# Low parts of the down-projection weights: from a VectorE subtraction to a ScalarE negation and an adding DMA

## The chip, the core and the metric

The kernel runs on one core of one Trainium2 chip. The metric is the device time of one execution in microseconds (us). Engines are named as in the profile: PE (TensorE, matrix products), DVE (VectorE), ACT (ScalarE), POOL (GpSimd) and SP (SyncE, which here issues the DMAs). PEld is PE's load of a stationary operand.

## What is computed

The reference is a trunk of two layers over 512 latent tokens and 256 context tokens with 1024 features, in float32. Each layer has three sub-layers: a SwiGLU feed-forward, a mixer (attention in layer 0, gated linear attention in layer 1) and a second SwiGLU. Cut to what matters here:

```
h = rms_norm(x, norm_g[i]) * (1 + scale) + shift
z = h @ w_gu                      # 1024 -> 2 * 2816
hid = silu(z_gate) * z_up         # 2816 hidden features
x = x + 0.5 * gate * (hid @ w_down)   # 2816 -> 1024
```

There are four such feed-forwards: ffn1 and ffn2 of layer 0, ffn1 of layer 1 (all three over 768 tokens), and ffn2 of layer 1 (over the 512 latent tokens only, the last stage of the kernel). The change concerns `w_down` alone.

## The kernel before, in words

**Numbers.** PE multiplies in a format (float32r) that keeps fewer bits than float32. Every operand is therefore split exactly into a high part `hi` (the value rounded to float32r) and a low part `lo = value - hi`, and each product is made of three: hi by hi, hi by lo, lo by hi (`pair`, L360, records them at L368). In the trace the weights are `whi` and `wlo`, the hidden operand is `dh` and `dl`, and the PSUM regions are `r`, `a` or `b`.

**Loading a weight unit.** `load_split` (L103) loads a unit in two halves. For each half, `raw` (L119) takes one of three buffers of the tag `raw` and issues the load from DRAM on SP's queue (L122). `split` (L125) then makes `whi` with a copy on ACT (L127) and `wlo` with a subtraction on DVE (L128). `whi` and `wlo` have three buffers each. These three rings of three buffers (`raw`, `whi`, `wlo`) are shared by all weights that pass through the feed-forward: a half can be loaded only when the `raw` buffer of three halves earlier has been read for the last time, and it can be converted only when PE has finished with the `whi` and `wlo` of three halves earlier.

**A feed-forward.** The 22 hidden tiles of 128 features are worked in four parts of 6, 6, 5 and 5 tiles (`PARTS`). In each part the gate and up products of its hidden tiles come first. From a hidden tile on that depends on the stage, they are made in seven products of halves (Strassen's form; `unit`, L612, matrix products at L596), whose weights go through the same rings in four pairs of buffers per tile. Then the part's down projection adds to the residual: four units of two halves (`load` at L531, used at L539), where a half holds 128 output features by 5 or 6 hidden tiles, that is 640 or 768 columns. In the first three parts each half is multiplied with all tokens at once. The fourth part is made by `close_out` (L396) in two passes over the tokens, so that the next norm can begin early: the first pass takes 256 tokens, with four units in order; the second pass takes the rest (512 tokens, in the last feed-forward 256), with the units in reverse order, of which the first is still there. So a close loads seven units, 14 halves. With three parts of eight halves before it, a feed-forward loads 38 halves, and the four feed-forwards load 152.

A half of the first pass of a close is only 15 products of 256 columns; a half of a main part is 36 products over 768 tokens (30 where the part has five tiles).

**Beside it.** DVE also adds the gated result to the residual (L392), forms the combinations of the seven products (L618, L633, L642, L652), and makes products for the modulation vectors of later sub-layers in the background (L291, with their own DMAs `wm<-w_mod`). ACT does the copies, Silu and the squares of the norm. POOL works in the two mixers only; it issues no DMA anywhere.

**The order of the work.** The program is written with a tile framework that places the waits. The order of instructions on each engine is not the order of the source: a planner simulates the time line with its own costs and takes what is ready, so a change of one operation's cost or engine can reorder others. Each engine and each DMA queue then works in its fixed order.

Of the kernel before, what the change touches and what calls it, by code (L numbers as in the profile page):

```python
# [14 lines left out]
ALU = mybir.AluOpType  # L15
# [12 lines left out]
ALL_SEGS = [(0, 256), (256, 512), (512, T)]  # context tokens, latent tokens  # L28
# [3 lines left out]
class Stage:  # L32
    """A sub-layer: loads its first weights, one unit after the other, then waits for its operand."""
# [14 lines left out]
class Net:  # L48
# [28 lines left out]
    # ---- the residual: four slots that hold other things inside a mixer, while it waits in DRAM --  # L77
# [25 lines left out]
    def load_split(self, src, n, pool=None, keep=4, slots=(None, None)):  # L103
        """n columns in two halves, each as (hi, lo)"""
# [13 lines left out]

    def raw(self, src):  # L119
        n = src.shape[-1]  # L120
        raw = self.stage.tile([128, 1024], F32, tag="raw", name="raw", bufs=3)[:, :n]
        self.nc.sync.dma_start(out=raw, in_=src)  # L122
        return raw

    def split(self, src, hi, lo, e=None):  # L125
        """src (float32, SBUF) -> hi + lo, both float32r"""
        self.nc.scalar.activation(out=hi, in_=src, func=AF.Copy)  # L127
        (e or self.nc.vector).tensor_tensor(out=lo, in0=src, in1=hi.bitcast(F32), op=ALU.subtract)  # L128

# [1 line left out]
    def rsqrt(self, out, v, shape):  # L131
        """out = 1/sqrt(v) for a small positive float32 tile"""
# [33 lines left out]
    def mod_finish(self, l, p):  # L166
        """bias; the scale piece becomes norm_g * (1 + scale), the FFN gates carry the 1/2"""
# [11 lines left out]
    def first_open(self, pool):  # L179
        """silu(c), silu(c_ctx) and zeros; the sum of four groups of 32 rows"""  # L180
# [14 lines left out]
    def first_product(self, pool, raw):  # L195
        """256 features of the vectors on the tensor engine, four products of 32 columns side by side"""
# [13 lines left out]
    def first_norm(self, pool, m, raw):  # L210
        """shift and scale of the first sub-layer, 128 features"""
# [7 lines left out]
    def first_gate(self, pool, i, raw):  # L219
        """half of the gate of the first sub-layer, 256 features"""  # L220
# [5 lines left out]
    def first_stats(self, pool):  # L226
        """1/rms of all tokens, on every partition"""
# [27 lines left out]
    def mod_queue(self, *pieces):  # L255
        """the products of the pieces (layer, number), in the two halves of the sums"""
# [6 lines left out]
    def mod_half(self, i):  # L263
        """a half of silu(c) and of silu(c_ctx) on every partition, for the background products"""
# [35 lines left out]
    def norm_squares(self, pool, seg, order=range(KT)):  # L300
        """sum over the features of a partition of the squares"""
# [13 lines left out]
    def norm_stats(self, seg, acc):  # L315
        """1/rms of each token of the segment, on every partition (PSUM)"""
# [36 lines left out]
    def mm3(self, out, w, x, first, last):  # L353
        """out += w^T x, w = (hi, lo) stationary, x = (hi, lo) moving"""
# [5 lines left out]
    def pair(self, w, nk, xk, segs, outs, cols=(0, 1)):  # L360
        """two column tiles of a weight unit, w[j] = (hi, lo) of [128, nk * 128], against the
        feature-major operand xk[k] = (hi, lo); outs[seg][j] are PSUM regions"""
# [9 lines left out]
    def regions(self, segs):  # L372
        """PSUM for two column tiles of each segment"""
# [22 lines left out]
    def close_out(self, load, nk, xk, segs, gate, nxt, off=0):  # L396
        """The last products of a sub-layer, in two passes over the weights: the norm of the first tokens runs
        under the products of the others, theirs under the first products of the next sub-layer, whose first
        weights come ahead of all that."""
# [46 lines left out]
    def ffn(self, l, sub, idx, segs, nxt, bg=(0, 0), first=4, start=False):  # L446
# [3 lines left out]
        # the first tiles: without the last segment, under the norm of it  # L450
# [9 lines left out]
        with st:  # L460
# [7 lines left out]
            def up(f, ss, regs=None):  # L468
                """the hidden tile f for the segments ss"""
# [13 lines left out]
            if start:  # L483
                # as the features come
# [28 lines left out]
            for pi, (f0, nf) in enumerate(PARTS):  # L513
# [17 lines left out]
                load = lambda u: self.load_split(dn[u], 2 * nf * 128)  # L531
# [14 lines left out]
    def seven_open(self, st, h, n0):  # L546
        """Gate and up columns (rows 1, 2) of a hidden tile against halves of the features and of the tokens,
        in seven products of halves in place of eight (Winograd's form of Strassen's)."""
# [50 lines left out]
        def start():  # L599
            """the place of the fourth block is free now"""  # L600
# [57 lines left out]
    def bcast(self, ap, n):  # L658
        """[128, a, b] -> [128, a, b, n] with a stride of zero"""
        return ap.unsqueeze(len(ap.shape)).to_broadcast(list(ap.shape) + [n])  # L660

    def rms_scale(self, pool, groups, shape, pool_squares=False):
        """1/rms of each group: groups = list of (ap [128, t, g, d], slice of the stats tile)"""
# [21 lines left out]
    def rope(self, pool, out, x, tab, nh, half):  # L685
        """x, out [128, nh, 2 * half] of one token tile; tab = (cos * gain, sin * gain) [128, 2 * half]"""
# [12 lines left out]
    def rot_tables(self, pool, nm, cos, sin, gain, d):  # L699
        """cos * gain and sin * gain, [128, 4, d]"""  # L700
# [14 lines left out]
    def pair_mixer(self, nxt, l=0):  # L715
        """Window attention of the first key/value head runs between the rest of the input projections,
# [1102 lines left out]
```

## Time and profile before

| | us |
|---|---|
| time, median of 3 runs | 2731.77 (2730.58 to 2735.99) |
| span of the profiled execution | 2731.1 |
| PE busy | 2639.5 (97%) |
| DVE busy | 2171.2 (80%) |
| ACT busy | 1197.9 (44%) |
| POOL busy | 170.3 (6%) |

The profiled execution's span, from its first to its last instruction, is 0.7 us below the median of the runs; its own device time is not listed apart. The busy share of PE counts modelled ends of pipelined matmuls, so the waits and the spacing of instructions say more than the share. The stages by time, in us from the span's start: start and ffn1 of layer 0 to about 572, attention mixer to about 1000, ffn2 of layer 0 and ffn1 of layer 1 to about 2066, gated linear attention and its projections to about 2412, ffn2 of layer 1 to the end. In each line of the trace, L12 is line 12 of the kernel; `out<-in` are the program's names.

### The profile page before, as it was taken

How to read it: one execution, taken by the hardware profiler on the slowest of the kernel's cores; microseconds unless marked ns; L12 is line 12 of the kernel's file. 1: busy time of each engine (PE TensorE's matmuls, PEld its weight loads, DVE VectorE, ACT ScalarE, POOL GpSimd, SP SyncE). 2: the span in 40 equal slices, each digit the busy share in tenths (PEclk: the TensorE clock that was granted, in tenths of full speed). 3: DMA queues.
4: the chain of work that ended last, by engine and by line, in shares of the span. 5: the costliest groups of instructions: out<-in, count | busy, mean ns of one | idle time of the engine just before them, and what ended most of it. 6: DMA issues, size and time to landing. Idle time of an engine off the chain costs nothing. (4 is left out here: it accounts for less than half of the span.)

```text
span 2731.1 us, 44146 instructions
## 1 busy us (share of the span) xinstructions
PE 2639.5 (97%) x16848; PEld 2450.8 (90%) x16848; DVE 2171.2 (80%) x4540; ACT 1197.9 (44%) x2254; POOL 170.3 (6%) x206
## 2 busy tenths in 40 slices
PE   7999999999978899999999999999999999899999
PEld 5899999989867789999999899999998999899899
DVE  5689798977788877797989877978777677778677
ACT  4324242445656753333324542424244555534444
POOL 0000000013344300000000000000000121000000
PEclk9999999999989999999999999999999999999999
DMA  8143444431000050433433314343233112422234
GB/s 311 41 144 119 137 132 143 132 126 31 24 24 1 1 170 24 126 120 122 130 124 110 126 47 144 100 149 105 91 105 102 55 63 70 147 64 97 96 108 130
DMA packets 103461, 279.30 MB, mean 102 GB/s; under 512 B 12146, under 2 KB 15090, under 8 KB 101714
## 3 DMA queue, kind: packets, MB, share of 16 engines
q1 hardware_dynamic: 103250, 276.49, 31.3%
q8 instruction: 132, 2.16, 0.3%
q14 instruction: 79, 0.65, 0.1%
HBM read 269.11 MB, written 7.34 MB: 101 GB/s over the span
## 5 line engine op out<-in xcount | busy, mean ns | idle before, releaser
L127 ACT ACTIVATE whi<-raw 128x512 fp32r<-128x512 f32 (+3 forms) x466 | 356.0, 767 | 730.7 <-PE r L368 324.2
L128 DVE TENSOR_TENSOR wlo<-raw,whi 128x512 fp32r<-128x512 f32 (+3 forms) x466 | 400.1, 861 | 72.3 <-ACT whi L127 69.7
L596 PE MATMUL r<-t,whi 128*128 128x384 f32 (+1 forms) x1704 | 401.2, 323 | 2.8 <-DVE u L633 2.0
L596 PE MATMUL r<-hh,wlo 128*128 128x384 f32 (+1 forms) x1136 | 366.3, 323 | 0.2
L596 PE MATMUL r<-hh,whi 128*128 128x384 f32 (+1 forms) x1136 | 365.8, 322 | 0.0
L596 PE MATMUL r<-hl,whi 128*128 128x384 f32 (+1 forms) x1136 | 365.8, 322 | 0.0
L291 DVE SCALAR_TENSOR_TENSOR junk<-wm,cb 128x512 bf16<-128x512 f32 x480 | 328.8, 685 | 13.1 <-ACT cb L270 8.0
L596 PEld LDWEIGHTS r<-t,whi 128*128 128x128 f32 x1704 | 295.6, 188 | 4.5 <-DVE u L633 2.8
L596 PE MATMUL r<-t,wlo 128*128 128x384 f32 (+1 forms) x852 | 273.3, 323 | 0.2 <-DVE wlo L128 0.2
L368 PE MATMUL r<-dh,whi 128*128 128x512 f32 (+1 forms) x952 | 267.3, 345 | 0.8 <-ACT whi L127 0.8
L368 PE MATMUL r<-dh,wlo 128*128 128x512 f32 (+1 forms) x952 | 266.8, 346 | 0.3 <-DVE wlo L128 0.3
L368 PE MATMUL r<-dl,whi 128*128 128x512 f32 (+1 forms) x952 | 266.8, 344 | 0.0
L127 ACT ACTIVATE whi<-s 128x512 fp32r<-128x512 f32 x284 | 174.9, 625 | 187.5 <-DVE s L618 75.2
L596 PEld LDWEIGHTS r<-hh,wlo 128*128 128x128 f32 x1136 | 213.4, 188 | 1.3 <-DVE wlo L128 1.3
L596 PEld LDWEIGHTS r<-hl,whi 128*128 128x128 f32 x1136 | 213.4, 188 | 0.8
L596 PEld LDWEIGHTS r<-hh,whi 128*128 128x128 f32 x1136 | 213.4, 188 | 0.3
L368 PEld LDWEIGHTS r<-dh,wlo 128*128 128x128 f32 x952 | 178.6, 188 | 24.3 <-DVE wlo L128 1.1
L368 PEld LDWEIGHTS r<-dh,whi 128*128 128x128 f32 x952 | 178.0, 188 | 24.5 <-ACT whi L127 2.7
L368 PEld LDWEIGHTS r<-dl,whi 128*128 128x128 f32 x952 | 178.1, 188 | 23.5
L128 DVE TENSOR_TENSOR wlo<-s,whi 128x512 fp32r<-128x512 f32 x284 | 190.6, 683 | 2.8 <-ACT whi L127 2.1
L392 DVE SCALAR_TENSOR_TENSOR x<-r,mod,x 128x512 f32<-128x512 f32 (+1 forms) x168 | 100.0, 631 | 87.3 <-PE r L368 86.9
L596 PEld LDWEIGHTS r<-t,wlo 128*128 128x128 f32 x852 | 159.9, 188 | 0.5 <-DVE wlo L128 0.5
(403 smaller groups left out, 5880.4 us busy)
## 6 DMA issues: line engine op xcount, KB each, us to landing
raw<-gu SPq DMA_DIRECT2D x176, 512.0 KB, 4.0
wm<-w_mod SPq DMA_DIRECT2D x240, 256.0 KB, 2.9
raw<-dn SPq DMA_DIRECT2D x88, 320.0 KB, 2.9
raw<-dn SPq DMA_DIRECT2D x64, 384.0 KB, 3.1
raw<-w_out SPq DMA_DIRECT2D x28, 512.0 KB, 3.7
m<-w_mod0a SPq DMA_DIRECT2D x12, 1024.0 KB, 10.2
raw<-w_in SPq DMA_DIRECT2D x8, 512.0 KB, 4.5
raw<-w_kq SPq DMA_DIRECT2D x8, 512.0 KB, 3.6
```

What stands on the lines that cost most here:

```text
L127: self.nc.scalar.activation(out=hi, in_=src, func=AF.Copy)
L128: (e or self.nc.vector).tensor_tensor(out=lo, in0=src, in1=hi.bitcast(F32), op=ALU.subtract)
L291: nc.vector.scalar_tensor_tensor(out=junk, in0=w, scalar=1.0, in1=self.cb[:, v, :], op0=ALU.mult, op1=ALU.mult, accum_out=self.acc[:, m, v ...
L368: nc.tensor.matmul(out=outs[s][j], lhsT=w[j][wi][:, k * 128:(k + 1) * 128], rhs=xk[k][xi][:, s0:s1], start=(k == 0 and i == 0), stop=(k == ...
L392: self.nc.vector.scalar_tensor_tensor(out=self.xs[m][:, s0:s1], in0=regs[s][j], scalar=gate[:, m, v:v + 1], in1=self.xs[m][:, s0:s1], op0= ...
L596: nc.tensor.matmul(out=o, lhsT=y[wi], rhs=x[k][xi], start=first and k == 0 and i == 0, stop=last and k == H - 1 and i == 2, skip_group_che ...
```

## The change

The down-projection weights are loaded by a new function, `load_parts`. It takes the same buffers, with the same three of each. The low part is now made by two steps: ACT writes `-hi` (a copy with scale -1.0) into the `wlo` buffer, and a DMA issued by POOL adds the raw weights to it in place, with both its source and its destination in SBUF. ACT then writes `hi` as before. The subtraction on DVE is gone for these halves; all other weights keep `load_split`. The remainder of the diff removes comments and docstrings.

```diff
+    def load_parts(self, src, n):
+        res = []
+        for j in range(2):
+            raw = self.raw(src[:, j * (n // 2):(j + 1) * (n // 2)])
+            hi = self.stage.tile([128, 1024], F32R, tag="whi", name="whi", bufs=3)[:, :n // 2]
+            lo = self.stage.tile([128, 1024], F32R, tag="wlo", name="wlo", bufs=3)[:, :n // 2]
+            self.split_by_dma(raw, hi, lo)
+            res.append((hi, lo))
+        return res
+
+    def split_by_dma(self, src, hi, lo):
+        nc = self.nc
+        nc.scalar.activation(out=lo, in_=src, func=AF.Copy, scale=-1.0)
+        nc.gpsimd.dma_start(out=lo, in_=src, accum_op=ALU.add)
+        nc.scalar.activation(out=hi, in_=src, func=AF.Copy)
...
-                load = lambda u: self.load_split(dn[u], 2 * nf * 128)
+                load = lambda u: self.load_parts(dn[u], 2 * nf * 128)
```

## Rows read from the trace of the kernel before

**Rows 1.** Page, part 1: busy us, share of the span, instructions.

```profile
span 2731.1 us, 44146 instructions
PE 2639.5 (97%) x16848; PEld 2450.8 (90%) x16848; DVE 2171.2 (80%) x4540; ACT 1197.9 (44%) x2254; POOL 170.3 (6%) x206
```

**Rows 2.** Stretches: busy us of PE, PEld, DVE, ACT, POOL; PE clock, DMA share, GB/s.

```profile
515.00:540.00 25.00, 23.25 (x148) 22.23 (x147) 22.22 (x52) 11.73 (x20) 0.00 (x0) 0.93 0.49 149
800.00:830.00 30.00, 20.00 (x95) 16.10 (x94) 29.73 (x82) 13.17 (x34) 15.93 (x16) 0.66 0.12 36
1120.00:1180.00 60.00, 60.00 (x346) 53.77 (x345) 47.16 (x105) 12.08 (x18) 0.00 (x0) 1.00 0.43 137
2704.00:2714.00 10.00, 10.00 (x87) 10.00 (x86) 7.05 (x13) 3.31 (x5) 0.00 (x0) 1.00 0.81 248
```

**Rows 3.** PE's waits for VectorE, whole span: us in total, times, longest.

```profile
PE b L368 <- DVE dl L128: 2.4, 4, 1.2
...
PE r L596 <- DVE u L633: 2.0, 3, 1.1
...
PE b L368 <- DVE hl L344: 1.6, 2, 0.8
```

**Rows 4.** Instruction groups by form: busy us, mean ns of one, idle before, releasers.

```profile
L128 DVE TENSOR_TENSOR wlo<-raw,whi 128x640 fp32r<-128x640 f32 x88 | 71.7, 820 | 19.7 <-ACT whi L127 18.9
...
L128 DVE TENSOR_TENSOR wlo<-raw,whi 128x768 fp32r<-128x768 f32 x68 | 65.1, 960 | 11.5 <-ACT whi L127 10.5
...
L127 ACT ACTIVATE whi<-raw 128x640 fp32r<-128x640 f32 x88 | 64.3, 738 | 144.5 <-PE r L368 61.9 <-PE r L596 32.6 <-PE b L368 20.1
...
L127 ACT ACTIVATE whi<-raw 128x768 fp32r<-128x768 f32 x68 | 57.2, 846 | 208.8 <-PE r L368 170.6 <-PE r L596 27.5 <-issue 7.3
```

**Rows 5.** ScalarE in order of time, second part of ffn2, layer 0: main halves.

```profile
1282.07 0.85 ACT L127 ACTIVATE whi<-raw 128x768 fp32r<-128x768 f32 x1 [5.43 <-PE r L368]
1288.35 0.85 ACT L127 ACTIVATE whi<-raw 128x768 fp32r<-128x768 f32 x1 [5.43 <-PE r L368]
```

**Rows 6.** ScalarE in order of time: second pass of the first close, then the last close.

```profile
554.09 0.74 ACT L127 ACTIVATE whi<-raw 128x640 fp32r<-128x640 f32 x1 [1.44 <-PE a L368]
...
557.57 0.74 ACT L127 ACTIVATE whi<-raw 128x640 fp32r<-128x640 f32 x1 [2.74 <-PE a L368]
...
2706.63 0.74 ACT L127 ACTIVATE whi<-raw 128x640 fp32r<-128x640 f32 x1 [1.53 <-DMA raw<-dn]
2708.80 0.74 ACT L127 ACTIVATE whi<-raw 128x640 fp32r<-128x640 f32 x1 [1.43 <-DMA raw<-dn]
2710.35 0.74 ACT L127 ACTIVATE whi<-raw 128x640 fp32r<-128x640 f32 x1 [0.81 <-DMA raw<-dn]
2714.56 0.74 ACT L127 ACTIVATE whi<-raw 128x640 fp32r<-128x640 f32 x1 [3.47 <-PE b L368]
2716.32 0.74 ACT L127 ACTIVATE whi<-raw 128x640 fp32r<-128x640 f32 x1 [1.03 <-PE b L368]
2718.09 0.74 ACT L127 ACTIVATE whi<-raw 128x640 fp32r<-128x640 f32 x1 [1.03 <-PE b L368]
```

**Rows 7.** DMA issues, KB each, us to landing, and the queue's share of 16 engines.

```profile
q1 hardware_dynamic: 103250, 276.49, 31.3%
...
raw<-dn SPq DMA_DIRECT2D x88, 320.0 KB, 2.9
...
x<-x_t SPq DMA_DIRECT2D x4, 768.0 KB, 7.5
...
ident<-ident SPq DMA_DIRECT2D x1, 64.0 KB, 2.3
```

**Rows 8.** The weight loads' issues on SP: duration ns min/median/max.

```profile
L122 SPq DMA_DIRECT2D raw<-dn x152: 327/328/383, 127.8 to 2718.1; - x152
```

**Rows 9.** VectorE and PE in order of time: main part's first half; two closes' second.

```profile
1258.47 0.95 DVE L128 TENSOR_TENSOR wlo<-raw,whi 128x768 fp32r<-128x768 f32 x1
...
1264.08 0.51 PE L368 MATMUL r<-dh,wlo 128*128 128x256 f32 x2
...
524.35 0.81 DVE L128 TENSOR_TENSOR wlo<-raw,whi 128x640 fp32r<-128x640 f32 x1
...
527.62 0.28 PE L368 MATMUL b<-dh,wlo 128*128 128x256 f32 x1
...
2696.96 0.82 DVE L128 TENSOR_TENSOR wlo<-raw,whi 128x640 fp32r<-128x640 f32 x1 [1.51 <-ACT whi L127]
...
2699.46 0.28 PE L368 MATMUL b<-dh,wlo 128*128 128x256 f32 x1
```

**Rows 10.** VectorE and PE in order of time: first half, part two, last feed-forward.

```profile
2531.18 0.96 DVE L128 TENSOR_TENSOR wlo<-raw,whi 128x768 fp32r<-128x768 f32 x1 [0.69 <-ACT whi L127]
...
2532.19 0.50 PE L368 MATMUL r<-dh,wlo 128*128 128x512 f32 x1 [0.26 <-DVE wlo L128]
```

## The prediction, made before the kernel was run

> **What bounds the kernel now.** I read the page first [rows 1]: PE 97% busy, DVE 80%, ACT 44%. That invites the thought that DVE is the next limit and that relief would help, so I then read stretches. In a down projection of ffn2, layer 0, PE is busy for all of 60.00 us at the full clock level (2.4 GHz), with DVE at 47 us; POOL executes nothing there [rows 2]. In the last close PE fills 10.00 of 10.00 us. PE is the bound in the feed-forwards, not by its busy share alone but because it has no gaps to give back. Third, PE's waits by releaser: over the whole span, its three longest groups of waits on DVE in the feed-forwards sum to 2.4 + 2.0 + 1.6 = 6.0 us [rows 3]. So 6 us is about all that a faster DVE can return to PE in the stages that change. What remains to be asked is how late a low part may come.
>
> **Removed.** Of 152 subtractions, 88 have 640 columns at 0.82 us and 64 have 768 at 0.96 us (four of the 68 in that row belong to another weight): 88 x 0.82 + 64 x 0.96 = 133.6 us of DVE [rows 4]. They lie beside PE's work. Up to 6.0 us return; I take half, -3, because the longest of the three groups waits for the hidden tile's own low part, which stays on DVE and only moves up its queue.
>
> **Added on ACT.** One more pass of the same size per half: 88 x 0.738 + 64 x 0.846 = 119.1 us [rows 4]. ACT idles 5.43 us before each main conversion [rows 5] and about 1 us in the close [rows 6], so the second pass, `hi`, runs beside the DMA: 0. Without that cover, were ACT full, each would cost its 0.74 to 0.85 us.
>
> **Added on POOL and the DMA engines.** 152 adding DMAs, each behind its ACT pass. POOL's queue is otherwise empty in these stages [rows 2], so nothing stands behind its waits except the next adding DMA. But a `raw` buffer is now held until the DMA has read it, and SP's queue, which waits for that buffer, has the following loads behind it. Call L the time from the end of the ACT pass to the moment when PE may use `wlo`. The trace has no adding DMA and none issued by POOL, so L must be bounded:
> - Low end 2.3 us: the 64 KB load, practically all fixed time [rows 7]. A gain below the old 0.8 us is excluded, since even that small DMA takes longer than the subtraction.
> - High end 7.5 us: 768 KB landing in the crowded start of the kernel [rows 7]; an adding DMA of 320 KB reads twice and writes once, 960 KB in all.
> - Taken: 4.2 us. The plain load of the same size takes 2.9 us. The queue moved 276.49 MB in 31.3% of 2731.1 us, so 320 KB (0.328 MB) occupy the engines for 0.328 / 276.49 x 854.8 = 1.0 us; I add that once for the second read, and 0.33 us, what one issue takes on SP [rows 8], for a start by software. 2.9 + 1.0 + 0.3 = 4.2. The nearest row is the plain load, hence so near to the low end.
>
> The Trainium skill, "DMA: Bandwidth & Descriptors", section Anatomy of one DMA, fits DMAs issued from GpSimd by 2.0 us plus bytes over 436 GB/s. By it a plain one of 320 KB would take an estimated 2.8 us, and the sum below would be +15 instead of +38; no run here shows it.
>
> **Where L is covered.** In main parts PE works 6.28 us on a half [rows 5] and two halves lie ready ahead: 12 us of cover, nothing to pay. The first half of a part has less: its subtraction starts at 1258.47 and PE takes the result at 1264.08 [rows 9], 5.6 us of cover, so it pays nothing at 4.2 either. In a close's first pass a half lasts 1.77 us (the spacing of the ACT passes in the last close, [rows 6]). There ACT already waits for the loads themselves (three rows released by the DMA of `raw`): the ring of three buffers is just fast enough. **One link of that ring**, from one load's issue to the issue into the same buffer three halves later, becomes 2.9 (load) + 0.74 (ACT) + L + about 0.2 (two hand-overs, my estimate from the 0.1 us steps between releaser and start) = 3.85 + L, against 3 x 1.77 = 5.3 us of PE work. Each link is late by L - 1.45.
>
> Counting halves from 0, the chain of releases runs through halves 1, 4 and 7. Half 1 has a lead: its low part now ends 2.5 us before PE takes it in the first close (524.35 + 0.81 to 527.62) and 1.7 us in the last (2696.96 + 0.82 to 2699.46) [rows 9]; with the 0.8 us that the subtraction took, it can bear L of 3.3 and 2.5. I take 3.4 for the three alike closes.
> - Three closes: (L - 3.4) + 2 (L - 1.45) = 3L - 6.3 each. Their second passes have 512 columns a product and 3.48 us a half [rows 6]; three halves take 10.4 us and cover the link up to L of about 6.4 (10.4 - 3.85 = 6.6, less a little for the next stage's loads).
> - The last close, 256 tokens in its second pass too, has two links more (halves 10 and 13): (L - 2.5) + 4 (L - 1.45) = 5L - 8.3.
> - The second and third parts of the last feed-forward: PE already waits for the first half's low part (0.26 us, [rows 10]). It bears only about 1.1 us: 2 (L - 1.1).
>
> Sum: 9L - 18.9 + 5L - 8.3 + 2L - 2.2 = **16L - 29.4**. At 4.2 it is 37.8; at 2.3 it is 7.4; at 7.5 it is 90.6 plus what is no longer covered (first halves of the other parts beyond 5.6, second passes beyond 6.4): writing out the releases half by half gives about 127.
>
> **The clock.** New gaps of 2.75 us may cost clock. In the first close, where PE idled 1.75 of 25 us, the granted clock averaged 0.93; in a mixer stretch with PE busy for 20 of 30 us it averaged 0.66, so a good part was at the lower level, 1.2 GHz [rows 2]. Bounds: 0, and 14.2 us of PE work per first pass at 0.66, which is 14.2 x (1/0.66 - 1) = 7.3 us, times 4 = 29. I take +3: PE's slower work falls mostly into waits that the ring imposes anyway.
>
> Total: 2731.8 + 37.8 - 3 + 3 = 2769.6, about **2770 us**. The durations are from one execution with a span of 2731.1 us, 0.7 below the median of 2731.77; I set the sum on the median.
>
> **Rivals.**
> - *Nothing to see*, 2734: the adding DMA is as quick as a small load, L near 2.3, so +7.4 less the 3 that DVE returns. For it: the data never leave SBUF, and the loads of 2.9 us contain a trip to DRAM. Against: two reads, and software on POOL. Within 0.2% (5.5 us, about what a measurement of this kernel can tell from no change) needs L of at most 2.4.
> - *Faster*, 2725: DVE's queue is what holds the closes; without the subtractions the hidden tile's and the norm's low parts come at once, and all 6.0 us return. Place: the first pass of each close. It decides only if L is at most 2.0, where the ring costs nothing. Against: [rows 7] show no transfer of this size under 2.9.
> - *POOL's issue is held up by DVE*, 2790 to 2830: the descriptors that POOL's program writes must wait for the DVE instruction in flight. DVE is busy for 7 of 10 us in the close [rows 2] with instructions of up to 0.96 us [rows 4], so L grows by up to one of them: 5.2 gives 16 x 5.2 - 29.4 = 53.8, hence 2786; two such waits, L of 6.1, give 2800, and more beyond 6.4. The Trainium skill, "SBUF — State Buffer", section Who interferes with whom, states such a lock, for VectorE operations with two ports (copy, cast, tensor_scalar); by that rule subtractions and gated adds, which fill the closes, would not block it. No run here shows the lock.
> - *The DMA engines are the limit*, about 2765 alone and more with a long L: in the close their share is already 0.81 [rows 2]. Load 1.0 + adding 2.0 = 3.0 us of all engines per half against 1.77 of PE: 1.25 us for 5 halves in three closes and for 11 in the last gives 32.5. It would look like a longer L, so I count it with the forecast.
> - *It doesn't do what it says*: an adding DMA that also converts float32 into float32r may move in tiny packets. L of 10 gives over 200 us: 2935 and up. The packets' sizes would tell.
>
> **How the numbers follow.** Forecast (L between 2.4 and 5, engines' load included) 0.60; held up by DVE or longer (5 to 8) 0.14; tiny packets 0.05; nothing to see 0.15; faster 0.06. So slower by over 0.2%: 0.79, same 0.15, faster 0.06. The likeliest case gives 2770. The range leaves out little of either end: from 2735 (L 2.4) to 2835 (L about 6.6, or 6 with clock losses); it leaves out faster, half of the nothing-to-see case and the longest L.
>
> **What would show it.** Right: DVE's subtractions on 640 and 768 columns gone, DVE busy lower by about 134 us and ACT higher by about 119; in each close, PE idle before L368 with the releaser DMA `wlo<-raw`, about 2.7 us at every third half; the main parts of the first three feed-forwards as dense as before; and a landing time of the adding DMA near 4.2 us. Wrong: landings at 2.4 us or less; PE waits that lie in the main parts or mixers; or closes no longer than before while the time grows elsewhere, which would mean that the planner's new order, not the DMA's delay, sets the time.

## The result, and the profile after

The changed kernel takes **2825.9 us** (median of 4 runs, 2824.5 to 2834.4) against 2731.2 us for the kernel before in the same comparison: ratio 1.035, 95% interval 1.033 to 1.037, 94.7 us slower. Forecast was 2770 us; the direction held and the time lies in the range, but the loss is two and a half times the forecast's 38 us.

The first three lines of the page of the changed kernel, its DMA queues and its issues (KB each, median us from issue to landing):

```profile
span 2822.7 us, 44596 instructions
...
PE 2666.8 (94%) x16848; PEld 2463.2 (87%) x16848; DVE 2053.6 (73%) x4388; ACT 1294.3 (46%) x2406; POOL 300.3 (11%) x358
...
q1 hardware_dynamic: 103250, 276.49, 30.1%
q0 software_dynamic: 21888, 54.01, 10.7%
...
raw<-dn SPq DMA_DIRECT2D x88, 320.0 KB, 3.2
wlo<-raw POOLq DMA_DIRECT2D x88, 320.0 KB, 4.5
...
wlo<-raw POOLq DMA_DIRECT2D x64, 384.0 KB, 5.4
```

Against [rows 1], DVE's busy time fell by 117.6 us, ACT's rose by 96.4, and PE's busy share fell from 97% to 94%. (ACT's added passes take 116.8 us, near the 119.1 forecast; the busy time counts once where instructions overlap.) The new queue, q0, is the adding DMA. Its 21888 packets carry 54.01 MB, 2.5 KB each, so the rival of tiny packets falls. But its packets take 10.7% of the sixteen DMA engines' 2822.7 us, over 152 DMAs: 2.0 us of all sixteen for each, twice the plain load's 1.0.

One line of source, L134 (the adding DMA), in the changed kernel, with what POOL waited for ahead of it:

```profile
L134 POOL DMA_DIRECT2D wlo<-raw x152: 850/859/1004, 144.2 to 2812.6; - x152
...
DMA to landing us min/median/max: 3.5/4.8/8.9
```

POOL starts 0.29 to 0.31 us after ACT's pass in 150 of 152 cases, read from the two engines' lines in order of time. At 52 of the 152 starts a DVE instruction was in flight, and POOL's own instruction took 0.85 to 1.00 us throughout. The rival in which DVE holds up POOL's issue falls too, and L is 0.29 + 4.76 = 5.05 us at the median, where 4.2 was taken.

PE's waits in the changed kernel (us in total, times, longest), the groups that the kernel before had not or had smaller [rows 3]:

```profile
PE b L386 <- DMA wlo<-raw: 26.1, 18, 3.6
...
PE r L614 <- DVE u L651: 10.6, 11, 1.7
PE r L614 <- ACT v L653: 7.0, 7, 2.6
...
PE r L386 <- DMA wlo<-raw: 5.2, 8, 1.2
PE a L386 <- DMA wlo<-raw: 5.1, 5, 1.5
...
PE a L341 <- DVE ss L330: 3.9, 2, 2.5
```

Waits for the adding DMA sum to 36.4 us. They don't make up 94.7. Of line 1, 18.9 us lie in the four first passes and 7.2 in the last close's second pass; line 5 is the second passes of the three other closes, line 4 the main parts, nearly all of it in the last feed-forward. So the closes hold 31.2 us of such waits. Lines 2, 3 and 6 are waits for ACT and DVE in the hidden tiles (L614) and in the norm of a close (L341): work that the change doesn't touch, and which only stands in the same queues.

To place the loss I cut PE's time line at the products with `wlo` of the down projections, and compared lengths with the kernel before (us; "tiles" are the stretches of hidden tiles and mixers up to a part's first product with `wlo`, "parts" the three main parts, then the two passes of the four closes, all summed). The mixers lie in the first column, where any new order of instructions shifts 2 to 6 us either way, so a few us there mean nothing. The cut goes by PE's products in order of time, and the planner moves products across it; what that does is said below the table. The other kernels are the experiments below.

```
                     tiles   parts   pass 1   pass 2
changed kernel       +29.0    +0.5    +38.5    +23.7
main_only            +44.0    +1.6     -0.3     -0.3
close_only            -8.1    -0.0    +39.7    +23.2
dve_add               +3.9    +1.1     +2.1    +12.4
more_buffers         +38.3    +2.8    +37.8    +16.1
four_buffers         +44.0    +0.9    +35.1    +14.0
plain                +13.1    -5.2    +23.9    +13.1
hold                  +9.9    -1.9    +11.1    +28.9
traffic               -6.4    +0.2     +8.0    +20.8
skip_last            +17.6    +1.2     -1.3     +0.6
raw_sg               +32.9    +1.5     -1.1     -0.5
pool_sub              +6.9    -5.7     -1.1     -0.1
```

The main parts are as long as before, nearly as forecast. The four first passes grew by 13.1, 8.6, 8.1 and 8.6 us, the second passes by 3.3, 7.6, 4.3 and 8.5. What no term of the forecast had is most of the first column: 29 us in the stretches between the parts.

Two cautions. While a low part is late, PE takes up products of the second pass before the first has ended; by its own last product the first pass grew by 13.8, 9.8 and 9.8 us in the three alike closes and the second by 2.6, 6.5 and 2.6. The two passes together (16.4, 16.2, 12.4 and 17.1 us) do not depend on the cut. And in the last feed-forward products of hidden tiles change sides: in the changed kernel 34 and 13 fewer lie inside its second and third part than before, in pool_last 24 and 22 fewer. There a shorter part beside a longer stretch of tiles is the same work, counted elsewhere.

ScalarE, POOL and PE of the second close, in order of time (start, us, what it is, idle before it and releaser):

```profile
1530.82 0.86 POOL L134 DMA_DIRECT2D wlo<-raw  x1 [3.30 <-ACT wlo L133]
...
1532.96 0.86 POOL L134 DMA_DIRECT2D wlo<-raw  x1 [1.27 <-ACT wlo L133]
...
1535.39 0.74 ACT L135 ACTIVATE whi<-raw 128x640 fp32r<-128x640 f32 x1 [1.47 <-PE b L386]
...
1536.03 0.72 ACT L133 ACTIVATE wlo<-raw 128x640 fp32r<-128x640 f32 x1
...
1537.05 0.86 POOL L134 DMA_DIRECT2D wlo<-raw  x1 [3.23 <-ACT wlo L133]
...
1542.42 0.38 PE L386 MATMUL b<-dh,wlo 128*128 128x256 f32 x1 [2.73 <-DMA wlo<-raw]
...
1547.87 0.39 PE L386 MATMUL b<-dh,wlo 128*128 128x256 f32 x1 [0.36 <-DMA wlo<-raw]
```

The DMA issued at 1537.05 for half 3 lands 5.3 us later, and PE, idle for 2.73 us, starts 0.04 us after it. The size is the forecast's (2.7 us), but by coincidence: this DMA took 5.3 us, and the wait is at half 3, not at halves 1, 4 and 7. Nor is it the forecast's ring of `raw`: ACT had waited for PE to give back the `whi` of half 0. Halves 4 to 6 also start within 0.3 us of a landing.

The ACT lines show something else that the forecast had the other way round. The program writes `-hi` (L133) and then `hi` (L135), but the planner put `hi` first in 134 of 152 halves: all 96 of the main parts and 38 of 56 in the closes. There `-hi`, and with it the adding DMA, starts 0.65 us later (median).

### The profile page after: what moved, and what is told of

Same layout as the page of the kernel before. It is cut to its first block, busy times and chain, and to the rows that moved or that the text cites. A ratio compares the mean times of both kernels' runs of the same rounds, so it can differ in the third digit from the quotient of the medians.

```text
span 2822.7 us, 44596 instructions
## 1 busy us (share of the span) xinstructions
PE 2666.8 (94%) x16848; PEld 2463.2 (87%) x16848; DVE 2053.6 (73%) x4388; ACT 1294.3 (46%) x2406; POOL 300.3 (11%) x358
## 3 DMA queue, kind: packets, MB, share of 16 engines
q0 software_dynamic: 21888, 54.01, 10.7%
## 5 line engine op out<-in xcount | busy, mean ns | idle before, releaser
L614 PE MATMUL r<-t,whi 128*128 128x384 f32 (+1 forms) x1704 | 403.6, 325 | 12.7 <-DVE u L651 10.6
L145 ACT ACTIVATE whi<-raw 128x512 fp32r<-128x512 f32 (+3 forms) x314 | 237.3, 757 | 325.6 <-PE r L614 84.2
L614 PE MATMUL r<-hh,whi 128*128 128x384 f32 (+1 forms) x1136 | 367.5, 324 | 7.1 <-ACT v L653 7.0
L614 PE MATMUL r<-hh,wlo 128*128 128x384 f32 (+1 forms) x1136 | 367.9, 324 | 0.6 <-DVE wlo L146 0.4
L614 PE MATMUL r<-hl,whi 128*128 128x384 f32 (+1 forms) x1136 | 366.5, 323 | 0.0
L134 POOL DMA_DIRECT2D wlo<-raw x152 | 130.9, 861 | 2041.3 <-ACT wlo L133 954.0
L146 DVE TENSOR_TENSOR wlo<-raw,whi 128x512 fp32r<-128x512 f32 (+3 forms) x314 | 267.1, 853 | 63.4 <-ACT whi L145 63.0
L614 PEld LDWEIGHTS r<-t,whi 128*128 128x128 f32 x1704 | 297.1, 189 | 16.9 <-DVE u L651 13.9
L614 PE MATMUL r<-t,wlo 128*128 128x384 f32 (+1 forms) x852 | 274.3, 324 | 0.0
L135 ACT ACTIVATE whi<-raw 128x640 fp32r<-128x640 f32 (+1 forms) x152 | 118.5, 781 | 310.3 <-PE r L386 107.6
L614 PEld LDWEIGHTS r<-hh,whi 128*128 128x128 f32 x1136 | 214.2, 189 | 10.0 <-ACT v L653 9.7
L614 PEld LDWEIGHTS r<-hh,wlo 128*128 128x128 f32 x1136 | 214.3, 189 | 2.5 <-DVE wlo L146 2.0
L614 PEld LDWEIGHTS r<-hl,whi 128*128 128x128 f32 x1136 | 214.4, 189 | 0.7
```

The lines of the kernel that those rows point to most:

```text
L134: nc.gpsimd.dma_start(out=lo, in_=src, accum_op=ALU.add)
L614: nc.tensor.matmul(out=o, lhsT=y[wi], rhs=x[k][xi], start=first and k == 0 and i == 0, stop=last and k == H - 1 and i == 2, skip_group_che ...
```

## Experiments

**Where: main_only and close_only.** The last parts keep one way of loading, the main parts the other.

```diff
-                load = lambda u: self.load_parts(dn[u], 2 * nf * 128)
+                load = lambda u, pi=pi: (self.load_split if pi == len(PARTS) - 1 else self.load_parts)(dn[u], 2 * nf * 128)
```

(close_only has the two names exchanged.)

> The adding DMA only in the three main parts of each feed-forward; the closes subtract on VectorE as before. Theory A (what costs is waiting for the DMA, place by place): the closes return to their old length and about 34 us remain, those that the changed kernel lost in the gate and up stretches ahead of the main parts: 2765 us, 2755 to 2775. Theory B (the planner's new order of instructions is what costs, and any use of the new split brings it): more than half of the 94.7 us stay, 2780 and up. Theory C (in main parts the delay is covered, as the prediction had it, and the stretches between them lose only what the closes throw out of step): 2725 to 2740.

Measured: 2772.3 us, ratio 1.015 (1.013 to 1.018).

> The adding DMA only in the closes; main parts subtract on VectorE. Theory A: the closes keep their loss of 38.4 us in the first passes and 23.7 us in the second: 2793 us, 2783 to 2803, and the gate and up stretches are as before. Theory B: 2780 and up too, but with losses outside the closes. Theory C: all of it is here, 2815 to 2830.

Measured: 2793.1 us, ratio 1.023 (1.020 to 1.025). Both came out as theory A said, and the table shows the losses place by place: the closes of close_only lose in sum what the changed kernel's closes lose, to within 1.2 us a column, and main_only loses only between its parts. The two nearly add up (1.5% and 2.3% against 3.5%).

**What of it is the DMA: dve_add.** Same two passes of ACT, the addition on DVE.

```diff
-        nc.gpsimd.dma_start(out=lo, in_=src, accum_op=ALU.add)
+        nc.vector.tensor_tensor(out=lo, in0=src, in1=lo.bitcast(F32), op=ALU.add)
```

> ScalarE writes -hi and hi as in the changed kernel, but VectorE adds raw to -hi in place, in everything: no DMA from GpSimd. Same extra 119 us of ScalarE and its place in the order, same 134 us of VectorE as before. Theory A (the DMA's delay): within 0.3% of the kernel before, 2728 to 2740; the close's first pass 16 to 18 us. Theory B (ScalarE's second pass and the order of the instructions): at least half of the 94.7 us stay, 2780 or more.

Measured: 2752.6 us, ratio 1.008 (1.005 to 1.011), between the two theories: some 22 us of loss need no adding DMA at all. Over half of it lies in second passes. (Here too `hi` stands first, in 138 of 152 halves.) PE and ACT of this run there, in order of time:

```profile
1519.77 0.72 ACT L135 ACTIVATE whi<-raw 128x640 fp32r<-128x640 f32 x1
1522.71 1.06 ACT L145 ACTIVATE whi<-raw 128x1024 fp32r<-128x1024 f32 x1 [2.22 <-DMA raw<-gu]
1523.67 0.71 ACT L328 ACTIVATE sq<-x 128x256 f32<-128x256 f32 x2
...
1528.20 1.02 PE L341 MATMUL a<-ones,ss 128*128 128x2 f32 x4 [6.32 <-DVE ss L330]
```

ACT idles for 2.22 us at a conversion of the next feed-forward, which waits for its load, while the norm's squares stand behind it in its fixed order; in the kernel before the squares came first. PE waits 6.32 us for their sum.

**Is it that order: dve_add_late.** The next stage's first loads are called one place later.

```diff
-                if nxt and (seg != segs[0] or i == 3):
+                if nxt and seg != segs[0]:
```

> VectorE adds raw to -hi, as in the run before (2752.6 us), and in the closes the next feed-forward's first loads and conversions stand behind the first pass's squares in the program, not ahead of them. Theory M (with ScalarE's second pass the planner puts conversions that wait for the next stage's loads ahead of the norm's squares, and TensorE waits for their sum, 6.3 and 4.0 us): these two waits go, 2738 to 2746. Theory N (the second passes are late because ScalarE and VectorE have more to do there): 2749 to 2756.

Measured: 2751.7 us, ratio 1.007 (1.005 to 1.009). The wait of 6.3 us became one of 2.7, that of 4.0 went, one of 1.0 is new, and second passes cost 4.9 in place of 12.4, as theory M said. Yet the time is in theory N's range and didn't move: the stretches of tiles lose 13.3 in place of 3.9, most of the difference in the two stretches with the mixers. So the order makes these waits; whether what came in their place is the same loss is not shown.

**Rings or engines: more_buffers, four_buffers, traffic.** more_buffers has five `raw` in three closes and six of each kind in the last; four_buffers has four of `raw` and `wlo` in all four closes.

```diff
+            own = self.ring and (self.last or i % 5 > 2)
+            if own:
+                raw = self.ring.tile([128, 640], F32, tag="raw", name="raw", bufs=6 if self.last else 2)
...
+            if self.ring and self.last:
+                hi = self.ring.tile([128, 640], F32R, tag="whi", name="whi", bufs=6)
+                lo = self.ring.tile([128, 640], F32R, tag="wlo", name="wlo", bufs=6)
```

> The changed kernel, with five raw buffers in place of three in the first three closes, and six of raw, whi and wlo each in the last. Theory A (ring of buffers held through the adding DMA): the last close falls from 46.3 us (both passes, 28.2 before) to about 31, only its first half being late; in the three others the ring of wlo remains (1.8 us of PE + 0.8 ScalarE + 5.1 to the landing = 7.7 per three halves against 5.3), so first passes fall from 24 to about 21; in all 2800 us, 2795 to 2812. Theory D (the DMA engines: load 1.0 us + adding 2.0 us of all of them per half against 1.77 of PE): the last close stays at 44 us or more, and the time at 2815 to 2830.

Measured: 2826.4 us, ratio 1.036 (1.033 to 1.039). The last close did fall, by 10.4 us to 35.9, less far than the ring alone would let it, and the hidden tiles before it lost 5.2 more. The other three first passes did not shrink (+14.9, +8.8, +9.2). The time is theory D's, the last close lies between the two theories.

> The changed kernel with four buffers of raw and four of wlo in every feed-forward's close, in place of three (raw alone at five changed nothing in the first three closes). Theory L (both rings bind: raw 2.9 + 0.7 + 0.3 + 4.8 + 0.2 = 8.9 us, wlo 1.8 + 0.8 + 0.3 + 4.8 = 7.7 us, against three halves of TensorE, 5.3; against four, 7.1): the first passes fall from 24 to 18 to 21 us, and the time to 2800 to 2813. Theory D (the DMA engines; the last close with six buffers went at 2.3 us a half): the first passes stay at 23 us or more, and the time at 2818 to 2830.

Measured: 2827.0 us, ratio 1.035 (1.033 to 1.036): theory L fell for the first three closes (+13.7, +8.8, +6.4), and the last close lost 11.6 in place of 17.1. `whi` kept three buffers in these closes in both runs, and the wait at half 3 above began with it: that ring was not tried there. What the buffers met is in the stretches. Columns: us of the stretch, busy us of PE, PEld, DVE, ACT, POOL, PE's clock, the DMA engines' share, GB/s. First the changed kernel's last close, then the same in more_buffers:

```profile
2772.00:2796.00 24.00, 16.24 (x122) 14.60 (x121) 4.44 (x9) 10.05 (x16) 6.88 (x8) 1.00 0.94 218
2796.00:2819.00 23.00, 15.49 (x120) 14.27 (x119) 3.77 (x9) 6.83 (x10) 4.30 (x5) 1.00 0.82 193
```

```profile
2785.00:2809.00 24.00, 20.47 (x145) 19.16 (x146) 3.50 (x8) 12.10 (x19) 8.03 (x10) 0.92 1.07 253
```

The engines' share is 0.94 already with three buffers, where it was 0.81 in the 10 us of [rows 2], and about 1 with six; most landings there lengthen to between 6 and 10 us. By packet times a half costs the engines 1.0 + 2.0 = 3.0 us, PE 1.77; a share of 1.07 says that packet times overlap, so the 3.0 is an upper bound. traffic was to test this without any dependency: the kernel before, with two idle copies of each `hi` in the closes.

```diff
+        res = self.load_split(src, n)
+        for hi, lo in res:
+            for _ in range(2):
+                keep = self.kpool.tile([128, 640], F32, tag="keep", name="keep")
+                self.nc.gpsimd.dma_start(out=keep, in_=hi.bitcast(F32))
```

> The kernel before, with VectorE's subtraction everywhere; in the closes GpSimd also copies each hi twice to a scratch in DRAM that nobody reads (1.1 us of all DMA engines each, by the copying run). These copies delay no raw and no wlo by a dependency; they only load the DMA engines: 1.0 + 2.2 = 3.2 us a half, about what the load and the adding DMA take (1.0 + 2.0). Theory Q (in the closes the DMA engines are the limit, which is why more buffers gave nothing): loads land late, first passes of 15 to 18 us grow by 4 us or more each, the last close by 8 or more; 2755 to 2795. Theory R (it is the rings alone): 2729 to 2740.

Measured: 2764.0 us, ratio 1.011 (1.009 to 1.014), in theory Q's range, but not at its places: the first passes grew by 4.7, 1.2, 0.9 and 1.1, not by 4 each; the second passes by 20.8. (By its own last product, the first pass of the three alike closes grew by 6.1, 5.0 and 3.4.) The copies were also lighter than I had reckoned (q0 took 3.5% of 2758.2 us for 112 of them, 0.86 us each). And there is a dependency after all: a copy reads `hi`, so it holds one of the three `whi` buffers until it lands, 5.6 us after its issue at the median, and ACT waits for that (us in total, times, longest):

```profile
ACT whi L144 <- DMA keep<-whi: 12.7, 8, 2.9
```

So the 29 us that the closes lose here are load on the engines and held buffers together. That the engines are near their limit is shown by the share and the landings of more_buffers; how much of the closes' loss is theirs and how much the rings' is not separated by any run.

**How long a DMA from POOL takes: plain and hold.** plain leaves out the addition (and so the low part).

```diff
-        nc.gpsimd.dma_start(out=lo, in_=src, accum_op=ALU.add)
+        nc.gpsimd.dma_start(out=lo, in_=src)
```

> The changed kernel with GpSimd's DMA copying raw to wlo instead of adding it (the low parts are then the raw weights: that step is left out). Theory J (a DMA from GpSimd takes that long whatever it does): landing 4.5 to 4.8 us after its issue at the median, as with the addition (4.76), and 2815 to 2828 us. Theory K (the second read and the addition cost over 1 us): landing about 3.4 us, as the copies of raw to DRAM took in the run that holds raw, and 2790 to 2805.

Measured: 2779.2 us, ratio 1.017 (1.016 to 1.019); the landing is 3.25 us at the median (4.76 with the addition), as theory K said, and the time fell below its range. Queue and issues of plain:

```profile
q0 software_dynamic: 21888, 54.01, 6.0%
...
wlo<-raw POOLq DMA_DIRECT2D x88, 320.0 KB, 3.2
```

6.0% of 2775.9 us over 152 is 1.1 us of the engines each, against 2.0: what a second read would add, though the queue's 54.01 MB are the same in both. 1.5 us less of landing, and half the engines' time with it, gave back 46.7 us; were it all the landing, 31 us for each us, where the forecast's sum has 16 L. hold keeps the subtraction on DVE and lets POOL copy `raw` away after `hi`.

```diff
+        nc.scalar.activation(out=src[:, 0:1], in_=src[:, 0:1], func=AF.Copy)
+        nc.vector.tensor_tensor(out=lo, in0=src, in1=hi.bitcast(F32), op=ALU.subtract)
+        keep = self.kpool.tile([128, 1024], F32, tag="keep", name="keep")[:, :src.shape[-1]]
+        nc.gpsimd.dma_start(out=keep, in_=src)
```

> VectorE subtracts as in the kernel before, in all down projections, but after hi GpSimd copies raw to a scratch in DRAM that nobody reads, so that raw is held through a DMA and wlo is not (ScalarE rewrites one column of raw with itself, so that the copy starts after it, as the adding DMA does). Theory E (a good part of the loss is that raw comes free late, and SP's in-order queue with it): the gate and up stretches lose again, over 15 of the 34 us, and the first passes of the closes over 10 of 38 us; 2760 to 2785. Theory F (only the lateness of wlo costs): 2727 to 2740.

Measured: 2777.7 us, ratio 1.016 (1.015 to 1.018). In theory E's range with 11.1 us in the first passes, but only 9.9 between the parts, not over 15, and 28.9 in the second passes, of which 15.0 are again PE's waits for the norm's sum. The time is half of the loss, but not by a held `raw` alone. The low parts came late too, for the subtraction waits for ACT's extra column, and PE for it:

```profile
PE b L389 <- DVE wlo L136: 7.2, 9, 2.6
```

And the copies load the engines (q0 4.9% of 2779.0 us, 0.9 us each). A held `raw`, the engines' load, this lateness and the new order are not told apart here.

**Between the parts: skip_last, skip_first, middle.** The adding DMA in main parts only, and not in the last, the first, or either of these loads.

```diff
+                load = lambda u, pi=pi: (self.load_parts if pi < len(PARTS) - 1 and u < 3 else self.load_split)(dn[u], 2 * nf * 128)
```

> The adding DMA only in main parts, and there not in the last of the four loads (which VectorE subtracts); with it in all four 2772.3 us. Theory G (at a part's end the next unit's raw loads wait for the buffers of the part's last halves, held through the adding DMA): most of the 45 us go, 2735 to 2750. Theory H (it is the first half's low part that comes late): 2765 to 2775. Theory I (in proportion to the number of adding DMAs, wherever they stand): 2758 to 2764.

> The adding DMA only in main parts, and there not in the first of the four loads. Theory G: 2755 to 2772. Theory H: most of the 45 us go, 2735 to 2750. Theory I: 2758 to 2764.

> The adding DMA only in main parts, and there in the second and third of the four loads alone, where 12 us of TensorE's work lie ahead of each half. Theories G and H together: the time of the kernel before or a little less, 2722 to 2735 (VectorE has 42 subtractions of 0.82 to 0.96 us less to do). Theory I: 2748 to 2754.

Measured: 2748.8 us, ratio 1.006 (1.004 to 1.008); 2766.0 us, 1.012 (1.010 to 1.013); 2738.0 us, 1.002 (1.001 to 1.004). (In middle 48 subtractions move, not 42.) The first two fit theory G, the third missed its range by 3 us. So more than half of the loss in main_only comes with the last load of a part; sparing the first returns about the quarter that its number of DMAs would; with both spared 5 us stay, and no gain. One path by which a part's end can hurt the next tiles: SP's queue, ScalarE, DVE and PE of main_only behind its second part:

```profile
318.99 4.05 SPq L303 DMA_DIRECT2D wm<-w_mod  x3
326.93 0.33 SPq L140 DMA_DIRECT2D raw<-gu  x1
...
332.10 1.77 SPq L287 DMA_DIRECT2D cb<-c_row  x2
...
337.12 1.06 ACT L288 ACTIVATE cb<-cb 128x1024 f32<-128x1024 f32 x1 [5.36 <-DMA cb<-c_row]
...
338.21 0.69 DVE L309 SCALAR_TENSOR_TENSOR junk<-wm,cb 128x512 bf16<-128x512 f32 x1 [3.55 <-ACT cb L288]
...
351.05 0.62 PE L614 MATMUL r<-t,whi 128*128 128x384 f32 x2 [0.73 <-DVE u L651]
```

The adding DMA issued at 319.92 landed at 326.86, and SP, which waited for its `raw` buffer, issued the tile's load at 326.93, where the kernel before did so at 322.38. The background vector `cb` came behind it in the queue, ACT waited for that, DVE for ACT (first at 338.21; in the kernel before, after a wait of 3.14 us for the same, at 336.71), and PE 0.73 us for DVE's sums. Of the 4.5 us at SP little is left at the end of this chain.

**Is it that raw buffer: raw_fourth, wm_two, raw_sg.** raw_fourth has a fourth `raw` for the last half of a part, with room made by two `wm` buffers in place of three; wm_two is its control. raw_sg takes the idle tile `sg` for that half instead.

```diff
+            if end and j:
+                raw = end.tile([128, T], F32, tag="sg", name="sg", bufs=1)[:, :n // 2]
+                self.nc.sync.dma_start(out=raw, in_=src[:, n // 2:n])
```

> A control for the next run: the adding DMA in main parts only (2772.3 us), with two buffers in place of three for the background weights wm, which makes room. All theories: 2768 to 2780.

> The control, and a fourth buffer of raw for the last half of each main part, so that the adding DMA of that half holds no buffer that the next hidden tile's loads need. Theory G (at a part's end those loads wait for raw held by the adding DMA): 15 us or more below the control, 2745 to 2760. Theory S (what costs there is the late wlo of the last halves, or the order of the queues): within 6 us of the control.

> The adding DMA in main parts only (2772.3 us), with the last half of each part loaded into sg, the buffer of the hidden tile, which is idle then, in place of a raw buffer; the background weights keep their three buffers. Theory G (SP's in-order queue waits at a part's end for a raw buffer held by the adding DMA, the background's loads behind it come late, VectorE waits for those, and TensorE for VectorE): 15 us or more lower, 2745 to 2757. Theory S (the late low parts of the last halves themselves, or the order of the instructions): 2766 to 2778.

Measured: wm_two 2791.0 us, 1.022 (1.019 to 1.025), outside what I took for certain: one background buffer less costs some 19 us on top of main_only. Its loads share SP's queue with the weights'; that this is why is not shown. raw_fourth 2797.1 us, 1.023 (1.021 to 1.026), against that control 6 us slower: inconclusive, with the control so disturbed. raw_sg 2771.1 us, 1.015 (1.013 to 1.016): 1 us from main_only and in theory S's range, so the buffer of the last half by itself is not it. In raw_sg SP issues the first load of the tile early (319.53) and then waits for a `wm` buffer until 325.28. There the wait taken from one place was met at the next. Which link carries the loss stays open; that more than half of it starts from the last load of a part is shown by skip_last.

**Can the relief of DVE be had: pool_sub and pool_last.** GpSimd subtracts, in main parts, or in three loads of the last feed-forward's main parts alone; no adding DMA.

```diff
-            self.split_by_dma(raw, hi, lo)
+            self.split(raw, hi, lo, self.nc.gpsimd)
```

> No adding DMA: hi from ScalarE, and in main parts GpSimd subtracts in VectorE's place (its subtraction of 384 columns took 1.01 us in the kernel before, so 1.7 and 2.0 us here); closes as before. Theory O (cover is what decides: 1 us later than VectorE, raw held 1 us longer, VectorE with 85 us less): 2722 to 2736. Theory P (any later low part at a part's ends throws the next units out of step): 2740 to 2755.

> No adding DMA anywhere; GpSimd subtracts in VectorE's place in the first three loads of the main parts of the last feed-forward alone, where with GpSimd's subtraction in all main parts the second and third part came out 3.6 and 3.1 us shorter. Theory O (relief of VectorE can be had where cover is long and nothing waits behind): 2724 to 2729. Theory P (what a part gains, the hidden tiles around it lose again, 3 to 4 us each there): 2729 to 2736.

Measured: pool_sub 2736.9 us, ratio 1.002 (1.000 to 1.003); pool_last 2731.6 us, 0.999 (0.998 to 1.000), no difference that can be told; pool_sub misses theory O's range by 1 us, pool_last is in theory P's. The last feed-forward's second and third part became 3.6 and 3.1 us shorter in both, and the tiles ahead of its three parts 3.3, 3.3 and 2.9 longer in pool_last. But this is mostly no gain given back, as theory P reads it: those two parts hold 24 and 22 products fewer, which now stand in the tiles ahead of them. At their usual spacing of 0.118 us they are 2.8 and 2.6 us, so at most 0.7 and 0.5 us of relief are left. No version here beats the kernel before.

## Why the prediction was right in direction and wrong in its sum

The forecast counted PE's waits for late low parts in the closes and at two parts of the last feed-forward, 37.8 us in all, and set everything else to nothing or let it cancel. The step that failed most is "nothing to pay" for the main parts: a held `raw` and the loads behind it were priced in the closes alone, and the stretches behind the main parts lost 29.0 us. "`hi` runs beside the DMA: 0" and the covered second passes failed too, and L was too short. That the measured time is inside the range is partly luck: the range was stretched for a longer L and for the clock, not for these steps. Nor does its upper end follow from its first reason: L of 6.6 gives 76.2 us by the formula, about 10 more for first halves beyond 5.6, so some 2820, not 2835.

- **The close's ring: the right place, the size partly by luck.** With the measured L of 5.05 the forecast's terms give 3 x 5.05 - 6.3 = 8.9 us for each of three closes and 5 x 5.05 - 8.3 = 17.0 for the last. The lengths fit: 13.1, 8.6, 8.1 in first passes, and 17.1 in both passes of the last. The waits for the adding DMA, which the terms stand for, do not: 6.9, 3.9, 3.9 and 11.4 us. The rest of the length is other waits (for the hidden tile's `dh` and `dl`, for `whi`), PE's slower spacing at 1.2 GHz, and products of the second pass done early. In the three alike closes the waits start at half 3 or 4, not at half 1. And the buffers show that the DMA engines are near their limit there; the sum could not tell the two, and "I count it with the forecast" hid that more buffers might not help.
- **L: too short.** 4.2 taken, 5.05 measured (5.7 for 768 columns). The term for the second read was 1.0 us, and the engines' time does rise by 0.9 over that of a plain copy from POOL; but the landing rises by 1.5 (from 3.25 to 4.76). POOL's own instruction is 0.33 us longer; what makes the rest is not shown. The Trainium skill, "DMA: Bandwidth & Descriptors", section Anatomy of one DMA, gave an estimate of 2.8 us for a plain one; the measured 3.2 is near, and the page's fit says nothing of the addition. At the forecast's 16 for each us this is 13.6 of the missing us.
- **"Their second passes ... cover the link": failed.** 15.2 us in the first three closes by the table (11.7 by each pass's own last product). PE waits there 5.1 us for the adding DMA, whose landings reach 8.1 us, so the link is not always covered, and 3.9 us for the norm's sum. dve_add, with no adding DMA, loses 12.4 in second passes by such waits: ACT's queue, where the next stage's conversions came to stand ahead of the norm's squares, is the second cause. The two are not measured apart.
- **"`hi` runs beside the DMA: 0": failed.** ACT's second pass was costed at its idle time, behind `-hi`. In 134 of 152 halves the planner put it ahead of `-hi`, so that the adding DMA starts 0.65 us later. dve_add, with both passes and no adding DMA, loses about 22 us. ACT has the time, 46% busy, but it takes its work in a fixed order, and the planner chose another one. What `hi` first costs by itself no run shows.
- **"nothing to pay" in the main parts: right for the parts, failed for what follows them.** The parts themselves became 0.5 us longer in sum, with 5.2 us of waits for the adding DMA in them and some products moved out. The tiles between lose 29.0, and 44.0 in main_only, where 7.9 (2 (L - 1.1)) was forecast. I had written that SP's queue has the following loads behind a held `raw`, and then priced it only in the closes. This is the largest step that failed; by which link the loss reaches PE stays open.
- **DVE's relief: hardly seen.** plain and pool_sub shorten the parts by 5.2 and 5.7 us, the changed kernel one part by 2.9, but these parts hold fewer products, which stand in the tiles beside them. In pool_last, where nothing else is late, at most 1.2 us in two parts are relief. The -3 of the sum is not shown.
- **The clock.** In the stretch of the second close the granted clock is 0.93, so for a part of it (3.4 us) PE ran at 1.2 GHz in place of 2.4, after the gap of 2.73 us above. Over the span PE's spacing in stretches granted half the clock exceeds its usual spacing by 36.0 us, before by 23.6: 12 us where 3 were taken, inside the bounds of 0 and 29. The lengths in the table contain it.
- **The lock between DVE and POOL: not seen.** Of the 52 starts with a DVE instruction in flight, 51 had a tensor_tensor or scalar_tensor_tensor, and POOL started 0.3 us after ACT all the same, but for two starts (0.97 and 2.25 us). This agrees with the Trainium skill ("SBUF — State Buffer", section Who interferes with whom), by which a copy stalls such a DMA and a tensor_tensor does not. Whether a copy on DVE would, no run here shows.

Split by the forecast's own terms, which is arithmetic on the table and not a measurement of causes, the missing 54 us are: 13.6 from L, 15.2 from the second passes of three closes, 21.6 between the parts, and 3.5 in the other terms of the closes (91.7 measured against 37.8 forecast, before the -3 and +3 that cancelled).

The second close's first pass and the start of its second, in the columns of [rows 2]:

```profile
1531.50:1556.00 24.50, 19.04 (x123) 16.80 (x122) 8.28 (x15) 12.18 (x21) 5.34 (x7) 0.93 0.89 204
```

PE is busy for 19.0 of 24.5 us and the DMA engines stand at 0.89; neither DVE (8.3) nor ACT (12.2) is short of time.

## What to carry to other kernels

A step that moves from an engine to a DMA should be priced by three things: its delay, the engines' time for every read and write of it, and how long it holds buffers for which an in-order queue waits. Where a kernel's rings are just fast enough, look past the stage that changes to the first loads of the next one; and before buffers are added, see whether the DMA engines' share leaves room for them. An idle engine does not make an added pass free: ask what stands behind it in that engine's order, and read from the trace which of two passes really goes first. And before a shorter stretch is called a gain, count its products.

## What the runs showed that I had not expected

- The addition nearly doubles the packets' time of a DMA inside SBUF (2.0 us against 1.1 for 320 to 384 KB) and adds 1.5 us to its landing; even POOL's instruction is longer, 0.86 us against 0.53.
- With six buffers in flight most landings stretch to between 6 and 10 us, while the share of the engines stands at about 1.
- The planner turned ACT's two passes round in 134 of 152 halves, and so put `hi` ahead of the pass that starts the DMA.
- One of three buffers of a background stream was worth some 19 us beside the adding DMA in main parts.
